# Taking all arithmetic off GpSimd in a three-block transformer kernel: rotation by transfers, probabilities on two engines, another order of gates

## The chip, the cores and the metric

The kernel runs on one core of a Trainium2 chip. A core has a matrix engine (TensorE, PE in the rows), a vector engine (VectorE, DVE), a scalar engine (ScalarE, ACT), GpSimd (POOL), and queues from which transfers between HBM and the on-chip memory are started; the queue of SyncE (SP) starts most of them. Each engine works through its own list of instructions in the order in which the program recorded them, and stands still when the instruction at the head of its list has to wait for another engine.

The metric is the time of one execution on the chip, in microseconds (us).

## The reference, cut to what matters

Three transformer blocks follow one another on a sequence of 512 tokens with 1024 features, all in fp32.

```python
# block 1: three branches on the normed input, mixed by gates
p = modulate(rms_norm(x, g1), sh1, sc1) @ w_in
q, k, v, a_dn, r, conv_in, sgu_in, gate_logit = split(p)
y_a = rms(gla_bidir(q, k, v, gates_f, gates_b, ...)) * silu(r) @ w_o_gla     # branch 0
y_b = silu(layer_norm(depthwise_conv(c1 * sigmoid(c2)))) @ w_o_conv          # branch 1
y_c = (su * spatial(layer_norm(sv))) @ w_o_sgu                               # branch 2
g = sigmoid(gate_logit)
x = x + g1 * ((g[0] * y_a + g[1] * y_b + g[2] * y_c) @ w_out);  x = x + g2 * swiglu(...)
# block 2, two layers
x = x + 0.5 * swiglu(x)
fq, fk, fv, ff, dq, dk, dv = split(rmsnorm(x) @ w_in)
o_f = softmax(fq @ fk.T / 8 + forget gates, causal) @ fv                     # 8 heads
dq, dk = rope(dq), rope(dk)          # t * cos + rotate_half(t) * sin
o_d = rms((softmax(dq1 @ dk1.T / 8) - lam * softmax(dq2 @ dk2.T / 8)) @ dv)  # 4 heads
x = x + concat(o_f, o_d) @ w_out;  x = x + 0.5 * swiglu(x)
# block 3: attention and a linear recurrence with gates side by side, then one projection
```

`rotate_half` takes the two halves of 32 features of a head and swaps them, with the sign of one turned.

## The kernel before, in words

**Layout.** Activations lie with features on the 128 partitions and the 512 tokens along the free axis, one buffer of 128x512 for 128 features (the names b in the rows). Each fp32 product is emulated by three passes on TensorE: an operand is split into a rounded part (hi) and the rest (lo), and hi·hi, hi·lo and lo·hi are added up in a PSUM bank (bk). `main_mm3` issues those three matmuls.

**The weight stream.** All weights come as 542 chunks of 128x1024 on the SP queue into `wraw` (three buffers). ScalarE casts a chunk into `whi`, and a subtraction, wraw − whi, makes `wlo`. It stands in `w_finish` (L506): on VectorE, or on GpSimd for chunks of odd number while `poolprep` is set, which it is in the two mixers of block 2 and in block 3.

**Main work and background work.** The recording code runs through the projections in order; these are the main matmuls. Everything else (gated linear attention, called GLA; attention heads; convolution; norms) is written as generators that are stepped (`tick`, L561) after each group of three main matmuls and put their own instructions in between. A generator stops at `sync()` (L430) until a modelled time has come, so that TensorE isn't given a matmul whose inputs are still being made. The modelled times come from `Clock` (L185): one clock for each engine, moved on by the `cost_*` functions (L209 to L237) whenever an instruction is recorded through the wrapper `Engine` (L241; all compute instructions therefore carry its line L260 in the profile). `idle()` moves TensorE's clock where no main matmul is left to put in. The order on each engine is thus fixed when the program is built, by the planner's costs; nothing is reordered on the chip.

**Block 1** (0 to about 860 us, then its feed-forward part until about 1396 us). `ORDER_1` (L1890) sets the order of main units: `r` are the inputs of GLA's output gate, `g` the gates of the three branches, `a` the rest of the modulation, `s` and `v` the two halves of the spatial branch, `between(b, ahead)` puts the products of branch b, each ahead of the gates of the next branch. GLA's heads (`gla_gate`, `gla_dir`, `gla_head`, L2051 to L2260) and the convolution (`conv_work`, L2275, one VectorE instruction for each of 31 taps of 8 buffers) are background work. The first product of branch 0 needs the last GLA head.

**Block 2's mixers** (`mixer2`, L1199; about 1600 to 1870 us and 2600 to 2870 us). `MIX_ORDER` runs the four differential heads (`diff(h)`), the values, and four pairs of forget-gate heads (`fox(j)`). `diff` makes q and k of a head: ScalarE copies four groups of 32 partitions out of PSUM to their rotated place (with the scale), VectorE multiplies the unrotated product by the cosines (`cosr`); later `rotated` (L1066) multiplies the rotated copy by the sines (`sinr`) on GpSimd and adds it there. `stack` (L774) splits the result and takes the low parts of each half-head (64 partitions) by subtractions on GpSimd. An attention head (`Pair`, L893) makes scores, exponentials, row sums, and in `probs` (L973) scales each row block by the reciprocal of its sum on VectorE; `turned` transposes and splits the probabilities, `products` multiplies with the values.

**Block 3** begins at about 3220 us and ends the program.

## Time and profile before

| what | us |
|---|---|
| median of 3 runs (3471.91 to 3474.83) | 3472.56 |
| the profiled execution | 3473.23 |
| its span | 3471.5 |

Over the span TensorE is busy 96%, VectorE 55%, ScalarE 40%, GpSimd 21%. These are averages over parts with very different loads, so the rows below go by stretch. A row of busy times by stretch reads: window in us from the start of the span, its length, then for PE, PEld (weight load), DVE, ACT and POOL the busy us and in brackets the instructions, then TensorE's granted clock as a share of full speed, the share of the transfer engines, GB/s. A row of waits reads: who waited, for whose result, us in all, times, the longest. A row of a group by shape reads: line, engine, operation, out<-in with shapes, count, busy us, mean ns, idle time before them and its releasers. A row of a tile reads: line, engine, operation, out<-in, count, duration in ns as shortest/median/longest. A row of the timeline or of the chain of waits begins with start and duration in us.

### The profile page before, as it was taken

To read this page: it belongs to the slowest core of one execution; us is meant where nothing else is said; L and a number is where in the kernel's file an instruction comes from. 1 tells how busy PE (TensorE), PEld (TensorE's weight loads), DVE (VectorE), ACT (ScalarE), POOL (GpSimd) and SP (SyncE) were. 2 spreads that over 40 slices of the span, in tenths; PEclk is the share of its full clock that TensorE was granted. 3 is DMA by queue.
4 is the path that set the end of the run, shared out by engine and by line. 5 is a ranking of instruction groups with operands and counts; after the bars stand their busy time and mean duration, and the time that the engine had idled before them with its cause. 6 is when DMAs were issued, how large, how long until landed. Compare 5 with 4: busy or idle time off the path is not lost.

```text
span 3471.5 us, 39465 instructions
## 1 busy us (share of the span) xinstructions
PE 3348.1 (96%) x15208; PEld 2757.0 (79%) x15208; DVE 1915.9 (55%) x3016; ACT 1373.7 (40%) x2220; POOL 718.9 (21%) x556
## 2 busy tenths in 40 slices
PE   7999989999999999999989999999999899999998
PEld 4887778887888888888767888888887678888787
DVE  5899887655333365433885443344334874433566
ACT  3325454333222332325864222222227753322465
POOL 0005221321000111104542110111017341111353
PEclk8999999999999999999999999999999999999999
DMA  5311115533222254332212222222332123222221
GB/s 199 103 67 60 50 68 187 177 115 106 96 97 97 93 171 159 102 115 97 67 61 86 97 96 97 92 97 97 112 109 76 43 76 107 97 94 95 79 85 49
DMA packets 110189, 345.00 MB, mean 99 GB/s; under 512 B 13424, under 2 KB 13680, under 8 KB 110000
## 3 DMA queue, kind: packets, MB, share of 16 engines
q1 hardware_dynamic: 84960, 296.78, 25.3%
q10 hardware_dynamic: 23760, 41.50, 3.8%
...
q14 instruction: 70, 0.57, 0.1%
...
## 4 chain that ended last, share of the span: by engine, by line
PE 48%; DVE 6%; ACT 3%; issue 1%; POOL 1%; POOLq 0%; DVEq 0%; ACTq 0%
PE bk L260 48%; DVE b L260 4%; ACT b L260 3%; DVE tinies L260 1%; DVE wlo L260 0%; ACT whi L260 0%; POOL b L260 0%; POOL wlo L260 0%; ACT L255 0%; POOLq L2841 0%; ACT bk L260 0%; ACT tinies L260 0%; DVEq L260 0%; DVE small L260 0%; ACTq L260 0%
## 5 line engine op out<-in xcount | busy, mean ns | idle before, releaser
L260 PE MATMUL bk<-b,whi 128*128 128x512 f32 (+1 forms) x8048 | 2504.9, 393 | 13.0 <-ACT b L260 7.6
L260 PEld LDWEIGHTS bk<-b,whi 128*128 128x128 f32 x8048 | 1504.9, 189 | 322.1 <-DVE b L260 10.2
L260 PE MATMUL bk<-b,wlo 128*128 128x512 f32 (+1 forms) x4024 | 1571.4, 391 | 13.5 <-DVE wlo L260 13.5
L260 POOL TENSOR_TENSOR b<-b,b 128x512 f32<-128x512 f32 (+2 forms) x381 | 527.3, 1392 | 2345.6 <-ACT b L260 1336.7
L260 DVE TENSOR_TENSOR wlo<-wraw,whi 128x1024 fp32r<-128x1024 f32 x495 | 648.2, 1311 | 529.7 <-ACT whi L260 528.7
L260 PEld LDWEIGHTS bk<-b,wlo 128*128 128x128 f32 x4024 | 760.3, 189 | 175.1 <-DVE wlo L260 16.5
L260 ACT CAST whi<-wraw 128x1024 fp32r<-128x1024 f32 x542 | 568.0, 1049 | 713.0 <-PE bk L260 416.3
L260 ACT CAST b<-b 128x512 fp32r<-128x512 f32 (+3 forms) x286 | 176.0, 619 | 521.3 <-POOL b L260 374.5
L260 DVE TENSOR_TENSOR b<-bk,b 128x512 f32<-128x512 f32 (+6 forms) x324 | 207.8, 657 | 251.5 <-PE bk L260 209.5
L260 DVE TENSOR_TENSOR b<-b,b 128x512 fp32r<-128x512 f32 (+3 forms) x250 | 180.9, 732 | 266.5 <-ACT b L260 264.0
L260 ACT ACTIVATE b<-b 128x512 f32<-128x512 f32 (+1 forms) x262 | 155.7, 607 | 295.7 <-DVE b L260 256.3
L260 DVE SCALAR_TENSOR_TENSOR b<-b,pvt,b 128x392 f32<-128x392 f32 (+7 forms) x296 | 237.3, 806 | 33.0 <-ACT b L260 26.4
L260 PE MATMUL bk<-whi,b 128*128 128x512 f32 x768 | 246.2, 396 | 2.6 <-ACT b L260 2.2
L260 PE MATMUL bk<-b,b 128*128 128x256 f32 (+6 forms) x1056 | 205.7, 337 | 28.3 <-DVE tinies L260 8.5
L260 PEld LDWEIGHTS bk<-b,b 128*128 128x128 f32 (+2 forms) x1056 | 171.9, 201 | 60.9 <-POOL b L260 17.4
L260 PEld LDWEIGHTS bk<-whi,b 128*128 128x128 f32 x768 | 146.0, 190 | 33.7 <-ACT b L260 2.7
L260 DVE SCALAR_TENSOR_TENSOR b<-b,small,b 128x512 f32<-128x512 f32 (+1 forms) x178 | 149.3, 840 | 19.5 <-ACT b L260 15.1
L260 POOL TENSOR_TENSOR wlo<-wraw,whi 128x1024 fp32r<-128x1024 f32 x47 | 118.0, 2510 | 202.3 <-ACT whi L260 170.7
L260 PE MATMUL bk<-cst,b 128*128 128x128 f32 (+1 forms) x776 | 112.7, 274 | 45.6 <-DVE b L260 38.1
L260 PEld LDWEIGHTS bk<-cst,b 128*128 128x128 f32 x776 | 98.5, 168 | 70.7 <-DVE b L260 50.0
L260 PE MATMUL bk<-wlo,b 128*128 128x512 f32 x384 | 151.0, 393 | 0.0
L260 ACT ACTIVATE b<-bk 128x512 f32<-128x512 f32 (+2 forms) x170 | 97.0, 571 | 106.0 <-PE bk L260 99.2
...
## 6 DMA issues: line engine op xcount, KB each, us to landing
wraw<-in_wst SPq DMA_DIRECT2D x542, 512.0 KB, 3.3
b<-in_ada1r ACTq DMA_DIRECT2D x64, 256.0 KB, 4.4
b<-in_ada ACTq DMA_DIRECT2D x48, 256.0 KB, 4.1
b<-in_ada SPq DMA_DIRECT2D x32, 256.0 KB, 5.3
xpark<-b ACTq DMA_DIRECT2D x16, 256.0 KB, 2.0
b<-xpark POOLq DMA_DIRECT2D x16, 256.0 KB, 5.6
b<-in_x SPq DMA_DIRECT2D x8, 256.0 KB, 5.7
b<-in_x ACTq DMA_DIRECT2D x8, 256.0 KB, 4.6
```

What stands on the lines that cost most here:

```text
L260: return f(*a, **kw)
```

## The change

No arithmetic is left on GpSimd. Every `nc.gpsimd` call that computes becomes the same call on VectorE: products and subtractions of GLA, the convolution's and the spatial branch's norms, sums of squares, `stack`, the product of the FFN, `poolprep`'s odd chunks (the switch is gone). Of its 560 rows GpSimd keeps 28: constants, memsets and the 16 transfers that bring x back. VectorE's instructions go from 3018 to 3534: 269 more of the kind b<-b,b 128x512, 80 of 64x512, 48 copies of 128x128, 47 chunks of `wlo`, 16 scalar-tensor-tensor with a PSUM operand (b<-bk,b, for the sines), 16 of 128x256 and some 60 small or single ones, less 22 scalings of probabilities. ScalarE's go from 2183 to 2136: 64 copies of 32x512 fewer, 22 scalings more. SP gets 64 transfers of 32x512 (64 KB each).

The rotation is now made after the sines: VectorE multiplies the product in PSUM by −s and the sines, four transfers move groups of 32 partitions to their rotated places, and a VectorE addition joins the two parts. `probs` gives a scaling to ScalarE where its modelled clock is behind VectorE's. The planner's clock no longer uses 0.5 for the two engines' sharing but 0.7, also for instructions that begin while the modelled GpSimd is busy. `ORDER_1` puts four gates of branch 2 ahead of branch 0's products. Block 3 waits with two kinds of unit until 8 buffers are free.

```diff
@@ class Clock
+        if shared and self.c["pool"] > t:
+            t += SHARED * min(self.c["pool"] - t, 1.4)
         self.c[name] = t + dur
         if name == "pool" and self.c["dve"] > t:
-            self.c["dve"] += 0.5 * min(dur, self.c["dve"] - t)
+            self.c["dve"] += SHARED * min(dur, self.c["dve"] - t)
...
+SHARED = 0.7
...
+    def copy_in(self, out, src):
+
+        t = self.clk.t
+        self.nc.sync.dma_start(out, src)
+        self.clk.t = t
+        return max(t, self.clk.now) + 2.2
...
-            eng = nc.gpsimd if self.poolprep and i % 2 else nc.vector
+            eng = nc.vector
             eng.tensor_sub(lo, src, hi.bitcast(F32))
...
-        nc.gpsimd.tensor_sub(lows[e].r[own[e] if keys else own[1 - e]], t.f[own[e]], out[e].f[own[e]])
+        k.nc.vector.tensor_sub(lows[e].r[own[e] if keys else own[1 - e]], t.f[own[e]], out[e].f[own[e]])
...
         for qb, o in part:
-            v = ss[0].f[:, o:o + qb * P + P]
-            ve.tensor_scalar(v, v, self.sm.f[:, 16 + qb:17 + qb], None, op0=ALU.mult)
+            v, r = ss[0].f[:, o:o + qb * P + P], self.sm.f[:, 16 + qb:17 + qb]
+            if k.clk.c["act"] < k.clk.c["dve"]:
+                k.act(v, v, AF.Copy, scale=r)
+            else:
+                ve.tensor_scalar(v, v, r, None, op0=ALU.mult)
...
@@ rotated
-        x, t = st["d" + name].pop(self.h)
-        yield from k.sync()
-        nc.gpsimd.tensor_mul(x.f, x.f, st["sinr"].f)
-        yield from k.sync()
-        nc.gpsimd.tensor_add(t.f, t.f, x.f)
+        x, t, at = st["d" + name].pop(self.h)
+        k.clk.t = max(k.clk.t, at)
+        yield from k.sync()
+        k.nc.vector.tensor_add(t.f, t.f, x.f)
...
@@ diff
-            x, t = k.blk(), k.blk()
-            for c in range(0, P, 32):
-                nc.scalar.mul(x.f[c:c + 32], b[c ^ 32:(c ^ 32) + 32], s)
+            y, x, t = k.blk(), k.blk(), k.blk()
+            nc.vector.scalar_tensor_tensor(y.f, b, -s, st["sinr"].f, op0=ALU.mult, op1=ALU.mult)
+            at = max(k.copy_in(x.f[c:c + 32], y.f[c ^ 32:(c ^ 32) + 32]) for c in range(0, P, 32))
             nc.vector.scalar_tensor_tensor(t.f, b, s, cosr.f, op0=ALU.mult, op1=ALU.mult)
             k.unbank(b)
-            st["d" + name][h] = x, t
+            k.free(y)
+            st["d" + name][h] = x, t, at
...
-ORDER_1 = (some("r", range(KT)) + some("g", range(KT), 0) + some("g", range(KT), 1) + some("a", [0]) + between(0, KT)
-           + between(1, KT) + some("v", range(2)) + some("s", range(KT)) + some("g", range(6), 2) + between(2, 6))
+ORDER_1 = (some("r", range(KT)) + some("g", range(KT), 0) + some("g", range(KT), 1) + some("a", [0])
+           + some("g", range(4), 2) + between(0, KT) + between(1, KT) + some("v", range(2)) + some("s", range(KT))
+           + some("g", range(4, 6), 2) + between(2, 6))
...
@@ gla_dir
-    nc.gpsimd.tensor_mul(qe.f, q.f, qe.f)
-    nc.gpsimd.tensor_mul(ke.f, kk.f, ke.f)
-    nc.gpsimd.tensor_mul(kd.f, kk.f, kd.f)
+    k.nc.vector.tensor_mul(qe.f, q.f, qe.f)
+    k.nc.vector.tensor_mul(ke.f, kk.f, ke.f)
+    k.nc.vector.tensor_mul(kd.f, kk.f, kd.f)
```

In the first mixer of block 2, GpSimd's list held, for the first differential head: the products with the sines, the two additions, one chunk of `wlo` and the four subtractions of `stack`.

```order
187 L260 TENSOR_TENSOR b_774_10300<-b_774_10300,b_770_10264 128x512
188 L260 TENSOR_TENSOR b_776_10339<-b_776_10339,b_770_10264 128x512
189 L260 TENSOR_TENSOR b_775_10301<-b_775_10301,b_774_10300 128x512
190 L260 TENSOR_TENSOR b_777_10340<-b_777_10340,b_776_10339 128x512
191 L260 TENSOR_TENSOR wlo_86<-wraw_80,whi_83 128x1024
192 L260 TENSOR_TENSOR b_780_10404<-b_775_10301,b_780_10404 64x512
193 L260 TENSOR_TENSOR b_781_10405<-b_775_10301,b_781_10405 64x512
194 L260 TENSOR_TENSOR b_784_10418<-b_777_10340,b_782_10416 64x512
195 L260 TENSOR_TENSOR b_785_10419<-b_777_10340,b_783_10417 64x512
```

In the changed kernel VectorE's list holds the same work at the same place. b_776 is the cosine part of q and b_779 that of k, b_775 and b_778 are the rotated sine parts that the transfers fill, and bk_66 is the next head's product.

```order
1464 L267 TENSOR_TENSOR wlo_88<-wraw_82,whi_85 128x1024
1465 L267 TENSOR_TENSOR b_776_10306<-b_776_10306,b_775_10305 128x512
1466 L267 SCALAR_TENSOR_TENSOR b_780_10381<-bk_66,b_770_10263 128x512
1467 L267 SCALAR_TENSOR_TENSOR b_782_10383<-bk_66,b_769_10262 128x512
1468 L267 TENSOR_TENSOR b_779_10346<-b_779_10346,b_778_10345 128x512
1469 L267 TENSOR_TENSOR wlo_86<-wraw_80,whi_83 128x1024
1470 L267 TENSOR_TENSOR b_783_10397<-b_776_10306,b_783_10397 64x512
1471 L267 TENSOR_TENSOR b_784_10398<-b_776_10306,b_784_10398 64x512
1472 L267 SCALAR_TENSOR_TENSOR b_789_10434<-bk_71,b_770_10263 128x512
1473 L267 SCALAR_TENSOR_TENSOR b_791_10436<-bk_71,b_769_10262 128x512
1474 L267 TENSOR_TENSOR b_787_10417<-b_779_10346,b_785_10415 64x512
1475 L267 TENSOR_TENSOR b_788_10418<-b_779_10346,b_786_10416 64x512
```

The additions and the subtractions now stand between weight chunks and the PSUM reads of the next head, in one list; the products with the sines have moved forward to the PSUM reads (rows 1466 and 1472).

On SP, which before had only weight chunks here, the rotation's transfers stand between the chunks.

```order
296 L257 DMA wraw_80<-in_wst 128x1024
297 L257 DMA b_775_10305<-b_774_10304 32x512 x4
298 L257 DMA wraw_81<-in_wst 128x1024
299 L257 DMA b_778_10345<-b_777_10344 32x512 x4
300 L257 DMA wraw_82<-in_wst 128x1024
301 L257 DMA b_781_10382<-b_780_10381 32x512 x4
302 L257 DMA wraw_80<-in_wst 128x1024
303 L257 DMA b_790_10435<-b_789_10434 32x512 x4
```

Each group of four waits for the product with the sines on VectorE, and the weight chunk behind it waits with it.

On TensorE at the end of GLA in block 1, before: the last transposes of a GLA head (128x128, with cst, the constants) stood directly ahead of branch 0's first product (bk_73<-b_203 and on, the output of GLA's head).

```order
1755 L260 MATMUL bk_71<-cst,b_259_3308 128x128 x2
1756 L260 MATMUL bk_71<-cst,b_266_3369 128x128 x2
1757 L260 MATMUL bk_67<-b_75_468,whi_85 128x512
1758 L260 MATMUL bk_67<-b_76_469,whi_85 128x512
1759 L260 MATMUL bk_67<-b_75_468,wlo_88 128x512
1760 L260 MATMUL bk_73<-b_203_2649,whi_83 128x512
1761 L260 MATMUL bk_73<-b_204_2650,whi_83 128x512
```

Now the same two transposes, and further down the first product (bk_70<-b_202). Between the two pieces stand 138 main matmuls.

```order
1714 L267 MATMUL bk_70<-cst,b_253_3207 128x128 x2
1715 L267 MATMUL bk_70<-cst,b_255_3257 128x128 x2
1716 L267 MATMUL bk_67<-b_65_325,whi_84 128x512
1717 L267 MATMUL bk_67<-b_66_326,whi_84 128x512
1718 L267 MATMUL bk_67<-b_65_325,wlo_87 128x512
```

```order
1852 L267 MATMUL bk_73<-b_75_468,whi_83 128x512
1853 L267 MATMUL bk_73<-b_76_469,whi_83 128x512
1854 L267 MATMUL bk_73<-b_75_468,wlo_86 128x512
1855 L267 MATMUL bk_70<-b_202_2601,whi_84 128x512
1856 L267 MATMUL bk_70<-b_203_2602,whi_84 128x512
```

The distance from the last transposes of this head to the product that needs its output went from three main matmuls to 138, of which the four gates make 96.

## Rows read from the trace of the kernel before

**Rows 1.** The page's line of busy time over the span.

```profile
PE 3348.1 (96%) x15208; PEld 2757.0 (79%) x15208; DVE 1915.9 (55%) x3016; ACT 1373.7 (40%) x2220; POOL 718.9 (21%) x556
```

**Rows 2.** Busy times by stretch; the columns are told above.

```profile
245.00:470.00 225.00, 202.55 (x963) 164.71 (x962) 201.41 (x261) 108.94 (x211) 89.25 (x72) 0.93 0.16 56
1600.00:1870.00 270.00, 247.81 (x1204) 204.01 (x1203) 193.97 (x462) 185.54 (x398) 132.69 (x103) 0.96 0.22 72
1870.00:2600.00 730.00, 730.00 (x3234) 605.00 (x3233) 282.72 (x318) 211.28 (x256) 79.57 (x60) 1.00 0.30 100
2600.00:2870.00 270.00, 242.75 (x1157) 199.03 (x1156) 188.22 (x456) 182.92 (x393) 131.39 (x102) 0.94 0.20 65
3360.00:3471.50 111.50, 98.22 (x479) 80.76 (x477) 73.75 (x180) 73.32 (x152) 44.73 (x41) 0.95 0.14 48
1700.00:1800.00 100.00, 86.50 (x457) 71.50 (x456) 86.55 (x266) 72.23 (x193) 39.69 (x42) 0.91 0.18 58
```

**Rows 3.** Waits of TensorE from 245 to 470 us.

```profile
PE bk L260 <- POOL b L260: 8.9, 5, 3.4
PE bk L260 <- ACT b L260: 7.8, 2, 7.4
```

**Rows 4.** Waits of TensorE from 1600 to 1870 us.

```profile
PE bk L260 <- DVE b L260: 17.4, 10, 6.2
```

**Rows 5.** Waits of TensorE from 2600 to 2870 us.

```profile
PE bk L260 <- DVE b L260: 15.6, 11, 2.9
PE bk L260 <- DVE wlo L260: 6.3, 3, 2.4
PE bk L260 <- DVE tinies L260: 5.1, 2, 4.9
```

**Rows 6.** Durations on VectorE, by tile, over the span (shapes at the end).

```profile
L260 DVE TENSOR_TENSOR b<-bk,b x324: 407/683/695, 177.4 to 3448.3; 128x512 f32<-128x512 f32 x109, 128x384 fp32r<-128x384 f32 x26, 64x512 f32<-64x512 f32 x12, 128x512 fp32r<-128x512 f32 x9
...
L260 DVE TENSOR_TENSOR wlo<-wraw,whi x495: 1160/1224/3190, 21.6 to 3436.3; 128x1024 fp32r<-128x1024 f32 x165
...
L260 DVE SCALAR_TENSOR_TENSOR tinies<-tinies,small x32: 210/562/2352, 1649.2 to 2736.5; 128x1 f32<-128x1 f32 x32
L260 DVE SCALAR_TENSOR_TENSOR b<-b,tinies,b x32: 351/750/2797, 1649.8 to 2736.8; 128x512 f32<-128x512 f32 x8, 128x384 f32<-128x384 f32 x8, 128x256 f32<-128x256 f32 x8, 128x128 f32<-128x128 f32 x8
```

**Rows 7.** Two groups of GpSimd by shape, over the span.

```profile
L260 POOL TENSOR_TENSOR b<-b,b 128x512 f32<-128x512 f32 x285 | 404.3, 1428 | 2013.8 <-ACT b L260 1032.6 <-DVE b L260 896.0 <-issue 57.9
...
L260 POOL TENSOR_TENSOR b<-b,b 64x512 fp32r<-64x512 f32 x80 | 107.6, 1346 | 44.5 <-ACT b L260 18.3 <-issue 16.4 <-PE bk L260 3.4
```

**Rows 8.** Timeline of VectorE from 2658 to 2673 us.

```profile
2659.95 1.33 DVE L260 SCALAR_TENSOR_TENSOR tinies<-tinies,small 128x1 f32<-128x1 f32 x1
2661.31 2.80 DVE L260 SCALAR_TENSOR_TENSOR b<-b,tinies,b 128x512 f32<-128x512 f32 x1
...
2670.81 1.43 DVE L260 SCALAR_TENSOR_TENSOR b<-b,tinies,b 128x128 f32<-128x128 f32 x1
```

**Rows 9.** Timeline of GpSimd from 2656 to 2673 us.

```profile
2656.59 4.67 POOL L260 TENSOR_TENSOR b<-b,b 128x512 f32<-128x512 f32 x3
2661.22 2.35 POOL L260 TENSOR_TENSOR wlo<-wraw,whi 128x1024 fp32r<-128x1024 f32 x1
2663.64 8.45 POOL L260 TENSOR_TENSOR b<-b,b 64x512 fp32r<-64x512 f32 x6
```

**Rows 10.** ScalarE's copies for the rotation, by shape, over the span.

```profile
L260 ACT ACTIVATE b<-bk 32x512 f32<-32x512 f32 x64 | 37.7, 589 | 4.1 <-PE bk L260 3.3
```

**Rows 11.** Transfers: kind, count, size of one, median us from issue to landing.

```profile
b<-xpark POOLq DMA_DIRECT2D x16, 256.0 KB, 5.6
...
b<-in_aup ACTq DMA_DIRECT2D x6, 64.0 KB, 2.1
```

**Rows 12.** Two pieces of the chain of waits in block 3's end.

```profile
3371.20 2.42 POOL wlo L260
...
3440.88 2.39 POOL wlo L260
```

More of the change, by code (lines that the diff above doesn't have):

```diff
@@ L197, in now, with add @@
         return self.c["pe"]
-    def add(self, name, dur):
+    def add(self, name, dur, shared=False):
         t = self.t - self.LAT if self.src == name else self.t
         t = max(self.c[name], t, self.c["pe"])
+        if shared and self.c["pool"] > t:
+            t += SHARED * min(self.c["pool"] - t, 1.4)
         self.c[name] = t + dur
         if name == "pool" and self.c["dve"] > t:
-            self.c["dve"] += 0.5 * min(dur, self.c["dve"] - t)
+            self.c["dve"] += SHARED * min(dur, self.c["dve"] - t)
         self.t = self.c[name] + self.LAT
@@ L238, in cost_pool, with in_psum @@
     return 0.06 + 1.0e-3 * width(out) if op == "memset" else max(0.5, 0.1 + 2.7e-3 * width(out))
+def in_psum(x):
+    return getattr(getattr(x, "tensor", None), "space", None) == bass.MemoryType.PSUM
 class Engine:
@@ L258, in g @@
                 out = a[0] if a else kw["out"]
-                self._clk.add(self._n, self._cost(op, out, a, kw))
+                shared = self._n == "dve" and not any(in_psum(x) for x in (*a, *kw.values()))
+                self._clk.add(self._n, self._cost(op, out, a, kw), shared)
                 return f(*a, **kw)
@@ L683, in feed @@
         else:
-            k.nc.gpsimd.tensor_add(self.acc.f, t.f, self.acc.f)
+            k.nc.vector.tensor_add(self.acc.f, t.f, self.acc.f)
             k.free(t)
@@ L746, in ffn @@
             k.unbank(pu)
-            nc.gpsimd.tensor_mul(u.f, t.f, u.f)
+            k.nc.vector.tensor_mul(u.f, t.f, u.f)
         hi, lo = k.rblk(), k.rblk()
@@ L925, in turned @@
         if c0:
-            nc.gpsimd.tensor_copy(hi.r[:, 0:c0], k.c("mask")[:, 0:c0])
-            nc.gpsimd.tensor_copy(lo.r[:, 0:c0], k.c("mask")[:, 0:c0])
+            nc.vector.tensor_copy(hi.r[:, 0:c0], k.c("mask")[:, 0:c0])
+            nc.vector.tensor_copy(lo.r[:, 0:c0], k.c("mask")[:, 0:c0])
         yield from k.sync()
@@ L973, in probs @@
     def probs(self, part, ss):
-        ve = self.k.nc.vector
+        k, ve = self.k, self.k.nc.vector
         rs = self.sm.f[:, 16 + part[-1][0]:17 + part[0][0]]
@@ L993, in finish @@
         if "ga" in st:
-            nc.gpsimd.tensor_mul(t.f, t.f, st["ga"][j].f)
+            k.nc.vector.tensor_mul(t.f, t.f, st["ga"][j].f)
             k.free(st["ga"][j])
@@ L1216, in mixer2 @@
     nc.scalar.dma_start(sinr.f, k.a["rope"][:, 1, :])
-    nc.gpsimd.tensor_mul(cosr.f, cosr.f, norm.bc)
-    nc.gpsimd.tensor_mul(sinr.f, sinr.f, norm.bc)
+    k.nc.vector.tensor_mul(cosr.f, cosr.f, norm.bc)
+    k.nc.vector.tensor_mul(sinr.f, sinr.f, norm.bc)
     z, t, cum = k.blk(), k.blk(), k.rblk()
@@ L1312, in out_proj @@
     k.drain()
-    k.poolprep = False
     for m in range(NOUT):
@@ L1370 @@
 H3 = 4
+NEED3 = 8
 def plan3():
@@ L1481, in feed @@
             else:
-                k.nc.gpsimd.tensor_add(parts[0].f, t.f, parts[0].f)
+                k.nc.vector.tensor_add(parts[0].f, t.f, parts[0].f)
                 k.free(t)
@@ L1528, in make @@
         if m % 2:
-            nc.gpsimd.tensor_mul(xa.f, xa.f, self.bc.f)
+            k.nc.vector.tensor_mul(xa.f, xa.f, self.bc.f)
         else:
@@ L1721, in lru_rest @@
         t = k.blk()
-        nc.gpsimd.tensor_mul(t.f, r.f, r.f)
+        k.nc.vector.tensor_mul(t.f, r.f, r.f)
         yield from k.sync()
@@ L1787, in lru @@
             r, i = gs
-            nc.gpsimd.tensor_mul(y.f, y.f, i.f)
+            k.nc.vector.tensor_mul(y.f, y.f, i.f)
             k.free(i)
@@ L1831, in block3 @@
     for kind, i in ORDER_3:
+        if kind in "sg":
+            k.need(NEED3)
         if kind == "x":
@@ L2083, in ctx_state @@
     last = t.f[:, 0:1] if s else t.f[:, n - 1:n]
-    nc.gpsimd.tensor_sub(w.f[:, 0:n], t.f[:, 0:n], last.to_broadcast([P, n]))
+    k.nc.vector.tensor_sub(w.f[:, 0:n], t.f[:, 0:n], last.to_broadcast([P, n]))
     k.act(w.f[:, 0:n], w.f[:, 0:n], AF.Exp, scale=-1.0 / 16)
-    nc.gpsimd.tensor_mul(w.f[:, 0:n], w.f[:, 0:n], st["ck"][h])
+    k.nc.vector.tensor_mul(w.f[:, 0:n], w.f[:, 0:n], st["ck"][h])
     yield from k.sync()
@@ L2159, in gla_dir @@
     f, l = pairs(kd.f)[:, :, s], pairs(qe.f)[:, :, 1 - s]
-    nc.gpsimd.tensor_mul(f, f, chunk[:, :, 1 - s:2 - s].to_broadcast([P, 4, 64]))
-    nc.gpsimd.tensor_mul(l, l, chunk[:, :, s:s + 1].to_broadcast([P, 4, 64]))
+    k.nc.vector.tensor_mul(f, f, chunk[:, :, 1 - s:2 - s].to_broadcast([P, 4, 64]))
+    k.nc.vector.tensor_mul(l, l, chunk[:, :, s:s + 1].to_broadcast([P, 4, 64]))
     yield from k.sync()
@@ L2230, in gla_head @@
     k.clk.t = old
-    nc.gpsimd.tensor_scalar(ss, ss, 1.0 / 256, EPS1, op0=ALU.mult, op1=ALU.add)
+    nc.vector.tensor_scalar(ss, ss, 1.0 / 256, EPS1, op0=ALU.mult, op1=ALU.add)
     k.rsqrt(y, ss, u)
@@ L2394, in sgu_norm @@
         v = t.f[:, 8 + tt:9 + tt]
-        nc.gpsimd.tensor_scalar(v, s.f[:, 13:14], EPS1, None, op0=ALU.add)
-        nc.gpsimd.tensor_copy(t.f[:, tt:tt + 1], s.f[:, 12:13])
+        nc.vector.tensor_scalar(v, s.f[:, 13:14], EPS1, None, op0=ALU.add)
+        nc.vector.tensor_copy(t.f[:, tt:tt + 1], s.f[:, 12:13])
         k.free(s)
@@ L2403, in sgu_norm @@
             nc.vector.tensor_scalar(x.f, x.f, t.f[:, tt:tt + 1], t.f[:, 16 + tt:17 + tt], op0=ALU.subtract, op1=ALU.mult)
-            nc.gpsimd.tensor_mul(x.f, x.f, st["lng"][half].f)
-            nc.gpsimd.tensor_add(x.f, x.f, st["lnb"][half].f)
+            k.nc.vector.tensor_mul(x.f, x.f, st["lng"][half].f)
+            k.nc.vector.tensor_add(x.f, x.f, st["lnb"][half].f)
             if tt % 2:
@@ L2427, in sgu_mix @@
     k.unbank(b)
-    nc.gpsimd.tensor_mul(su.f, t.f, su.f)
+    k.nc.vector.tensor_mul(su.f, t.f, su.f)
     k.free(t)
@@ L2677, in product @@
         else:
-            nc.gpsimd.tensor_add(yacc[m].f, yacc[m].f, g.f)
+            k.nc.vector.tensor_add(yacc[m].f, yacc[m].f, g.f)
             k.free(g)
```

11 lines of the change are left out of this document (4 added, 7 removed).

## The prediction

> **What bounds the kernel now.** I read the busy line first: TensorE works 3348.1 of 3471.5 us, so 123.4 us are idle, and no other engine comes near it [rows 1]. Then the busy times by stretch, because an average over parts with different limits tells nothing of a change in some of them [rows 2]. From 1870 to 2600 us (feed-forward work) TensorE is busy all 730 us at a granted clock of 1.00: there a moved instruction on another engine can cost or gain nothing as long as its results come in time. The idle time lies in GLA (245 to 470 us: 225 − 202.55 = 22.5 us), the two mixers (270 − 247.81 = 22.2 and 270 − 242.75 = 27.3) and the end of block 3 (111.5 − 98.22 = 13.3). It costs more than itself: the granted clock there is 0.93, 0.96, 0.94 and 0.95 as a mean of the levels 1.2 and 2.4 GHz, it falls after idle time, and a stretch with mean c loses up to (1 − c) of its busy time beside the idle time. With that, GLA loses 22.5 + 0.07 × 202.55 = 36.6 us, the mixers 22.2 + 0.04 × 247.81 = 32.1 and 27.3 + 0.06 × 242.75 = 41.8, the end 13.3 + 0.05 × 98.22 = 18.2: 128.7 us that other engines' work can change. The first 245 us hold nothing that the edit touches much, and I leave them and the short remaining stalls out.
>
> Last I read whom TensorE waits for there. In GLA: GpSimd 8.9 us in five waits, ScalarE 7.8 in two, one of them 7.4 [rows 3]. In the first mixer VectorE's b for 17.4 of the 22.2 us [rows 4], in the second VectorE for 15.6 + 6.3 + 5.1 = 27.0 of 27.3 [rows 5]. So in the mixers GpSimd is not what TensorE waits for by name; the edit adds work to the engine that is.
>
> **Why moving work onto the waited-for engine can help.** VectorE is slow there for a reason that leaves with GpSimd. An operation that reads PSUM takes 683 ns at the median and never more than 695 [rows 6]. One that reads only on-chip memory varies: a chunk of wlo 1160 at the least and 3190 at the most, the one-column product that prepares a differential head's probabilities 210 to 2352, the wide one behind it 351 to 2797 [rows 6]. A stretch of the second mixer shows when [rows 8, 9]: from 2659.95 to about 2672 VectorE runs four such pairs, with only two short reciprocals between them; the eight operations add up to 12.0 us (1.33 + 2.80 for the first pair; the last operation, 128x128, takes 1.43), while GpSimd works without a break for 15.5 us (4.67 + 2.35 + 8.45). Alone the pairs would take 4 × 0.21 + (0.75 + 0.62 + 0.49 + 0.35) = 3.1 us by the shortest and middle durations of rows 6 (0.62 and 0.49 are interpolated by width). GpSimd's ten operations there are priced on VectorE at 3 × 0.69 + 1.22 + 6 × 0.69 = 7.4 us (0.69 for 512 columns, whatever the partitions; 1.22 for a chunk). Both engines together thus need 10.5 us in one list where they took 12.0 side by side.
>
> The Trainium skill (SBUF — State Buffer, "SBUF: two separate sides") says that VectorE and GpSimd share a port pair which one instruction holds to its end, among others for a VectorE operation with two on-chip inputs against a GpSimd one that reads on-chip memory. By that rule operations of two on-chip inputs should stretch and those with a PSUM input not, and the trace agrees (up to 3190 against at most 695 ns [rows 6]).
>
> **The change part by part.**
>
> *Moved arithmetic.* GpSimd's mean for 128x512 is 1428 ns and for 64x512 1346 [rows 7]; on VectorE 690, a ratio of 0.48 to 0.51; a chunk 2.35 [rows 9] against 1.22. At 0.49 the first mixer's 132.69 us of GpSimd [rows 2] become 65 us of VectorE, the second's 131.39 become 64, GLA's 89.25 become 44, the end's 44.73 become 22. Against that goes the relief. It is at least nothing, and at most the example's rate, 8.9 us of excess in 15.5 us of GpSimd = 0.57, for all of GpSimd's time, 76 us in a mixer. Much of VectorE's work there reads PSUM and is not relieved, so I take 0.3: 40 us in a mixer, 27 in GLA, 13 in the end. VectorE's busy time then goes to 194 + 65 − 40 = 219 and 188 + 64 − 40 = 212 of 270 us, in GLA to 201 + 44 − 27 = 218 of 225, and in the end to 83 of 111.5. GLA is the tight one; its fill was 201.41 / 225 = 0.90 already. Its operations there are scans and taps of the convolution which fill in whatever time is left and are due later (the second half of block 1), so I let it slip rather than stop.
>
> *Rotation.* 64 copies of ScalarE go, 37.7 us in all [rows 10], 19 us in each mixer; the two GpSimd products for q and k of a head become 16 VectorE operations with a PSUM operand, 16 × 0.69 = 11 us, 5.5 in each mixer (they don't suffer contention, and the additions and the subtractions of the halves are in the 65 us above). The 64 transfers of 64 KB are new between weight chunks on SP. The nearest rows: 64 KB from HBM land in 2.1 us, 256 KB from the place where x is parked in 5.6 [rows 11]. The planner counts on 2.2. So each of 16 additions comes between 0 and 5.6 − 2.2 = 3.4 us late, 0 to 54 us for VectorE's list, since everything behind a waiting addition waits, the chunks' subtractions among them. I take 0.5 us each, 8 us, near the row of the same size, and half of it at TensorE: +4. A group of four that waits for its product holds back the next weight chunk on SP by as long; three chunks are in buffers, so I cost that at nothing, and if the buffers run dry it would show as waits for whi.
>
> *Probabilities.* 22 of 104 scalings go to ScalarE, 0.42 us each at the median shapes: less than 5 us per mixer off VectorE, on an engine that gets 19 us free. Part of what hides the rotation's 5.5.
>
> *Order of gates.* Between the last GLA transposes and the first product that needs GLA's output stand 138 main matmuls instead of three. At 730 / 3234 = 0.226 us [rows 2] that is 31 us of cover, where ScalarE's 7.4 us wait [rows 3] and those behind it now fall. What is late next is the convolution, whose taps share VectorE with the moved work; its products come at the end of branch 0's. I charge +3 (between 0 and its own share of one such wait, 7.4).
>
> *Block 3's buffers and the end.* The wait for eight buffers only moves units behind others; nothing by itself. Two chunks on GpSimd stand on the chain of waits, 2.42 and 2.39 us [rows 12]; on VectorE 1.22 each.
>
> **The sum.** GLA: the 8.9 us of waits for GpSimd go, with the clock that hangs on idle time 8.9 × 36.6 / 22.5 = 14.5, and half of ScalarE's 7.8, 3.9: −18. Mixers: the example's 12.0 us become 10.5 if all moved work stands ahead of the result that is waited for (12% less) and 3.1 if none does (74%). I take 35%, below the middle, because VectorE's fill goes up to 0.8: 32.1 × 17.4 / 22.2 × 0.35 = −9 and 41.8 × 27.0 / 27.3 × 0.35 = −14.5. The end: a third of 18.2, −6, of which the two chunks are 2.4. Together −47.5; +4 +3 of new waits: −40.5. From the profiled execution's 3473.2 that is 3432.7; the median of the runs lies 0.7 below that execution, so 3432.
>
> **The rivals.**
>
> *A, VectorE becomes the bound of the mixers (slower).* If the relief is near nothing, the first mixer's list holds 194 + 65 + 5.5 − 4.6 = 260 us and the second's 188 + 64 + 1 = 253. The highest fill that a stretch of rows 2 shows is 0.90; the mixers then take 260 / 0.90 = 289 and 281 us, +19 and +11. Less GLA's 14.5, with nothing won at the end: +15.5, 3488. It decides from the point where VectorE's busy time in a mixer exceeds 243 us (0.90 × 270), that is with a relief under about 15 us; for it speaks that in the dense 100 us from 1700 VectorE is busy 86.55 already, more than TensorE's 86.50 [rows 2]; against it the stretched durations of rows 6. The skill speaks for A (Perfetto Trace Analysis, "Optimizing Scalar/DVE Operations"): between GpSimd and VectorE, which share a port, moving operations might not help. By that sentence alone the sum would be that of A or C; the trace shows up to 2.6 times the duration for a chunk beside GpSimd [rows 6], and I hold with the rows.
>
> *B, late transfers.* At the upper bound of 54 us on VectorE, half at TensorE, +27 in place of +4: 3455. For it: SP's queue also carries 512 KB chunks; against: transfers are busy 0.20 to 0.22 of the time in the mixers [rows 2].
>
> *C, the waits change owner only.* GpSimd's waits become VectorE's of the same length: 3472 within 7 us.
>
> *D, most of it goes.* Of the 128.7 us the mixers' relief reaches 74% of its waits and GLA's stalls go with the 31 us of cover: 0.74 × (25.2 + 41.3) + 36.6 + 9 = 95, 3378.
>
> **How the numbers follow.** Forecast 0.46 (3405 to 3455), A 0.17, B 0.12, C 0.11, D 0.14. A difference under 0.2%, 7 us, can't be told from none. Faster: forecast, B and D, 0.72; same: C, 0.11; slower: A, 0.17. The range goes down to 3388, which leaves out half of D, and up to 3483, which leaves out two thirds of A.
>
> **What would show it.** Right: wlo and the wide products [rows 8] at their shortest durations with hardly any spread; GpSimd's waits gone; VectorE's busy time in the mixers near 215 us and the mixers 10 to 15 us shorter; no wait of TensorE of 5 us near the end of GLA. Wrong: VectorE over 243 us of 270 in a mixer (A); VectorE idle for transfers ahead of the 16 additions by more than a microsecond each (B); a convolution that comes late by over 10 us in block 1; waits of the old length under VectorE's name (C).

## The result, and the profile after

The changed kernel takes 3415.11 us (median of 4 runs, 3414.29 to 3416.99), the one before 3472.23 beside it: a ratio of 0.9835 with a 95% interval of 0.9822 to 0.9848, 57 us faster where 40 were forecast. The time lies inside the range, and the forecast case was the one that came; but two of its terms, the rotation and block 3, came out with the wrong sign, as the runs below show.

The page's line of busy time of the changed kernel, against [rows 1]:

```profile
PE 3324.9 (97%) x15208; PEld 2741.6 (80%) x15208; DVE 2042.5 (60%) x3532; ACT 1348.2 (39%) x2173; POOL 9.3 (0%) x24
```

Stretches are cut at the starts of the same weight chunks' subtractions. In the mixers that is the same work on TensorE as in [rows 2] (1204 and 1157 matmuls); GLA's stretch holds 1032 where it held 963, because background work falls elsewhere. Busy times of the changed kernel by stretch: GLA, first mixer, the feed-forward work between, second mixer, the end of block 3.

```profile
249.00:463.00 214.00, 205.34 (x1032) 169.69 (x1032) 182.78 (x323) 113.54 (x231) 0.00 (x0) 0.99 0.17 57
1579.00:1831.00 252.00, 242.06 (x1204) 199.41 (x1203) 210.83 (x556) 169.57 (x372) 4.37 (x8) 0.99 0.26 84
1831.00:2559.00 728.00, 728.00 (x3225) 603.14 (x3224) 314.17 (x377) 210.26 (x253) 0.00 (x0) 1.00 0.30 100
2559.00:2799.00 240.00, 230.78 (x1157) 190.61 (x1156) 205.28 (x550) 165.40 (x366) 4.36 (x8) 0.99 0.26 83
3308.00:3414.00 106.00, 87.27 (x421) 72.31 (x419) 78.32 (x197) 64.76 (x138) 0.00 (x0) 0.91 0.14 50
```

TensorE's idle time fell from 22.2 to 9.9 us in the first mixer and from 27.3 to 9.2 in the second, and the granted clock there went from 0.96 and 0.94 to 0.99. The end went the other way: 18.7 us idle at 0.91. The last window of the end in [rows 2] begins earlier; cut at the same chunk, the kernel before had 13.3 us idle there, at 0.94:

```profile
3371.00:3471.50 100.50, 87.22 (x428) 71.53 (x427) 71.63 (x172) 62.58 (x135) 37.26 (x35) 0.94 0.15 53
```

In the first mixer VectorE does more work (210.8 us of 252, against 194.0 of 270) and yet is waited for less. Its durations show why; by tile, against [rows 6]:

```profile
L267 DVE TENSOR_TENSOR wlo<-wraw,whi x542: 1161/1225/1227, 21.4 to 3394.4; 128x1024 fp32r<-128x1024 f32 x181
...
L267 DVE SCALAR_TENSOR_TENSOR tinies<-tinies,small x32: 213/219/223, 1620.3 to 2669.8; 128x1 f32<-128x1 f32 x32
L267 DVE SCALAR_TENSOR_TENSOR b<-b,tinies,b x32: 350/552/752, 1620.5 to 2670.1; 128x512 f32<-128x512 f32 x8, 128x384 f32<-128x384 f32 x8, 128x256 f32<-128x256 f32 x8, 128x128 f32<-128x128 f32 x8
```

The longest chunk went from 3190 to 1227 ns, the longest small product from 2352 to 223. TensorE's waits in the first mixer of the changed kernel, against [rows 4], and in GLA, against [rows 3]:

```profile
PE bk L267 <- DVE b L267: 8.9, 9, 4.5
PE bk L267 <- DVE wlo L267: 0.6, 1, 0.6
PE bk L267 <- ACT b L267: 0.3, 1, 0.3
```

```profile
PE bk L267 <- DVE b L267: 7.8, 8, 2.2
PE bk L267 <- ACT b L267: 0.8, 1, 0.8
```

And the transfers that VectorE waits for, over the span (all waits of its own operations for the rotation):

```profile
DVE b L267 <- DMA b<-b: 1.7, 3, 1.3
```

### The profile page after: what moved, and what is told of

Same layout as the page of the kernel before. It is cut to its first block, busy times and chain, and to the rows that moved or that the text cites. A ratio compares the mean times of both kernels' runs of the same rounds, so it can differ in the third digit from the quotient of the medians.

```text
span 3414.0 us, 39098 instructions
## 1 busy us (share of the span) xinstructions
PE 3324.9 (97%) x15208; PEld 2741.6 (80%) x15208; DVE 2042.5 (60%) x3532; ACT 1348.2 (39%) x2173; POOL 9.3 (0%) x24
## 5 line engine op out<-in xcount | busy, mean ns | idle before, releaser
L267 DVE TENSOR_TENSOR wlo<-wraw,whi 128x1024 fp32r<-128x1024 f32 x542 | 661.5, 1222 | 554.5 <-ACT whi L267 552.6
L267 DVE TENSOR_TENSOR b<-b,b 128x512 f32<-128x512 f32 (+4 forms) x615 | 407.6, 672 | 183.3 <-ACT b L267 149.3
L267 ACT ACTIVATE b<-b 128x512 f32<-128x512 f32 (+2 forms) x261 | 155.1, 608 | 280.5 <-DVE b L267 268.2
L267 DVE SCALAR_TENSOR_TENSOR b<-b,pvt,b 128x392 f32<-128x392 f32 (+7 forms) x296 | 204.9, 696 | 32.0 <-ACT b L267 25.5
L267 PE MATMUL bk<-b,b 128*128 128x128 f32 (+6 forms) x1056 | 191.8, 320 | 17.5 <-DVE b L267 9.6
L267 PEld LDWEIGHTS bk<-b,b 128*128 128x128 f32 (+2 forms) x1056 | 159.2, 188 | 44.1 <-ACT b L267 13.7
L267 DVE SCALAR_TENSOR_TENSOR b<-b,small,b 128x512 f32<-128x512 f32 (+1 forms) x178 | 133.5, 750 | 22.3 <-ACT b L267 19.0
L267 PEld LDWEIGHTS bk<-cst,b 128*128 128x128 f32 x776 | 98.7, 168 | 50.8 <-DVE b L267 34.5
L267 ACT COPY b<-bk 128x512 f32<-128x512 f32 (+5 forms) x130 | 65.7, 535 | 118.1 <-PE bk L267 116.9
L267 ACT ACTIVATE b<-b,tinies 128x512 f32<-128x512 f32 (+3 forms) x182 | 100.3, 560 | 29.3 <-DVE tinies L267 29.0
L267 DVE TENSOR_TENSOR b<-b,bk 128x512 f32<-128x512 f32 x64 | 43.9, 686 | 110.2 <-PE bk L267 102.9
```

Of the source, the lines that this page charges most:

```text
L267: return f(*a, **kw)
```

## The experiments

The table has the length of each stretch in the profiled execution of each kernel, in us, from the start of one chunk's subtraction to that of another (chunks counted from 0; the last column of stretches goes to TensorE's last matmul), and the median of its runs. Two kernels with the same lists in a stretch differ there by up to 2.6 us (175.7 and 178.3 in block 3), so smaller differences say nothing, and a sum of two stretches is uncertain by more. In GLA's stretch the kernels with the arithmetic on VectorE run some 64 more matmuls than the others (1032 and 968 in arith_only and before), so against the kernel before only the sum of the first two columns is to be read.

| kernel | GLA 32–55 | 55–120 | mixer 251–282 | mixer 416–445 | block 3 507–533 | end | median |
|---|---|---|---|---|---|---|---|
| before | 224.7 | 399.8 | 270.3 | 270.3 | 168.8 | 96.5 | 3472.2 |
| changed | 214.0 | 389.7 | 251.6 | 240.2 | 177.9 | 101.4 | 3415.1 |
| arith_only | 213.9 | 402.8 | 262.5 | 255.5 | 175.7 | 97.0 | 3450.8 |
| rot_only | 222.9 | 400.4 | 264.0 | 250.7 | 169.0 | 96.6 | 3447.3 |
| order_only | 223.1 | 403.0 | 270.4 | 270.2 | 168.7 | 96.5 | 3474.8 |
| old_order | 213.5 | 402.8 | 251.2 | 241.3 | 176.1 | 101.1 | 3430.0 |
| old_rot | 213.5 | 391.3 | 264.9 | 256.1 | 175.8 | 102.0 | 3444.0 |
| old_probs | 213.5 | 388.2 | 254.4 | 243.0 | 177.9 | 98.7 | 3417.1 |
| beside | 213.5 | 389.8 | 278.5 | 267.4 | 176.6 | 102.1 | 3471.0 |
| beside_write | 213.5 | 388.1 | 254.4 | 243.2 | 175.7 | 101.9 | 3419.8 |
| act_load | 213.5 | 389.8 | 256.7 | 246.9 | 178.3 | 101.3 | 3429.3 |
| rot_act | 213.5 | 389.7 | 267.5 | 258.9 | 176.5 | 101.2 | 3449.3 |
| gp_lru | 213.4 | 388.2 | 251.0 | 241.3 | 169.4 | 95.6 | 3404.8 |
| best | 213.9 | 389.8 | 251.7 | 241.7 | 169.6 | 95.2 | 3402.4 |

**1. Only the moved arithmetic (arith_only).** The parts that are undone, against the changed kernel:

```diff
-            at = max(k.copy_in(x.f[c:c + 32], y.f[c ^ 32:(c ^ 32) + 32]) for c in range(0, P, 32))
+            for c in range(0, P, 32):
+                nc.scalar.mul(x.f[c:c + 32], b[c ^ 32:(c ^ 32) + 32], s)
...
-           + some("g", range(4), 2) + between(0, KT) + between(1, KT) + some("v", range(2)) + some("s", range(KT))
+           + between(0, KT) + between(1, KT) + some("v", range(2)) + some("s", range(KT))
...
-            if k.clk.c["act"] < k.clk.c["dve"]:
...
-            k.need(NEED3)
```

> The changed kernel with three parts undone and block 3's wait for buffers left out: rotation by ScalarE's copies again (its product and addition on VectorE), all probabilities on VectorE, the old order of gates. So of the change only the move of GpSimd's arithmetic to VectorE is left. Theory of relief (VectorE is stretched by GpSimd's work beside it, and that ends): the two mixers, 541 us together before and 492 in the changed kernel, come to 490 to 510; wlo at 1160 to 1230 ns; the whole at 3425 to 3440. Rival (rotation by transfers and the split of probabilities make the mixers shorter by taking work from ScalarE): the mixers stay at 530 or more, the whole at 3450 or more.

3450.79 us, ratio 0.9934 (0.9919 to 0.9949). The mixers took 518.0 us: 22.6 less than before, not 30 to 50. Neither theory's figure for the mixers was met, and the whole just reaches the rival's 3450: relief is real (no chunk takes longer than 1228 ns here), and is less than half of the mixers' 48.8.

**2. Idle GpSimd work beside (beside).**

```diff
             eng.tensor_sub(lo, src, hi.bitcast(F32))
+            if self.beside:
+                g, u = self.raw.gpsimd, self.load
+                g.tensor_mul(u[:, 0:1], hi[:, 0:1].bitcast(F32), u[:, 0:1])
+                for _ in range(3):
+                    g.tensor_mul(u, u, u)
```

> The changed kernel with idle work on GpSimd in block 2's mixers: behind each chunk of weights, once it is prepared, one product of one column that reads whi and three products of 128x512 in a buffer of its own, that nobody reads; about 4.3 us per chunk, 31 and 29 chunks, some 130 us in each mixer, as much as GpSimd had before. The lists of all other engines are those of the changed kernel. Theory of relief: wlo and the wide products stretch again (wlo to 2 us and more at the longest), VectorE's busy time in a mixer grows by 20 to 40 us and each mixer by 10 to 30; the whole 3435 to 3475. Rival (the gain came from the other order of the lists): VectorE's durations grow but the mixers stay within 5 us each, the whole under 3425.

3470.99 us, all that the change had won; the mixers 54.1 us longer with the same lists. The theory of relief has its direct proof: nothing but GpSimd's work was added. The chunk's durations, by tile, and GpSimd's own work by shape:

```profile
L267 DVE TENSOR_TENSOR wlo<-wraw,whi x542: 1161/1225/2060, 21.2 to 3446.8; 128x1024 fp32r<-128x1024 f32 x181
```

```profile
L541 POOL TENSOR_TENSOR load<-load 128x512 f32<-128x512 f32 x186 | 233.3, 1254 | 14.6
```

That it costs more here than moving the arithmetic won is no contradiction: VectorE carries the moved work as well, which I take for the reason; no run tests it.

**3. Idle GpSimd work that reads nothing (beside_write).**

```diff
-                for _ in range(3):
-                    g.tensor_mul(u, u, u)
+                for _ in range(7):
+                    g.memset(u, 0.0)
```

> As the kernel with idle work on GpSimd beside the mixers, but instead of three products of 128x512 behind each chunk seven fills of 128x512 with a constant, which read no buffer. Theory (what stretches VectorE is that both engines read on-chip memory): wlo stays at 1230 ns and the mixers within 5 us of the changed kernel, the whole under 3425. Rival (any GpSimd work beside stretches VectorE): wlo to 1.8 us or more, the mixers longer by 20 us or more together, the whole over 3435.

3419.76 us; the mixers 5.8 us longer than in the changed kernel, a little over the bound expected. GpSimd was as busy as in the run before it (229.8 against 233.3 us), and no chunk was stretched:

```profile
L267 DVE TENSOR_TENSOR wlo<-wraw,whi x542: 1159/1225/1228, 22.0 to 3398.2; 128x1024 fp32r<-128x1024 f32 x181
```

```profile
L541 POOL MEMSET load<- 128x512 f32 x434 | 229.8, 530 | 25.1
```

So it is not GpSimd's being busy that stretches VectorE, but its reading. Another rival falls with it: in both runs ScalarE's next cast sometimes waits until the idle work lets a `whi` buffer go, and it waits longer in the cheap run (36.7 us) than in the dear one (20.1). The Trainium skill says the same (SBUF — State Buffer, "SBUF: two separate sides"): a VectorE operation with two on-chip inputs contends only with a GpSimd operation that reads on-chip memory. The two runs agree with it.

**4. The rotation undone (old_rot)**, the first edit of experiment 1 alone, with the product with the sines and the addition on VectorE.

> The changed kernel with the rotation alone undone (64 ScalarE copies, product with the sines and addition on VectorE). Theory of relief: VectorE has the same number of operations, ScalarE 19 us more in each mixer; the mixers longer by 0 to 8 us together, the whole 3415 to 3424. Rival (the transfers carry the mixers' gain): mixers longer by 20 us or more, the whole over 3435.

3443.99 us, the mixers 29.2 us longer: the rival's figure. The rotation, which I had priced at +4, carries as much of the mixers' gain as the relief, or more. TensorE waits little for ScalarE by name here, so I looked one step back, at what VectorE waits for. From 1597 to 1717 us, where the differential heads are made:

```profile
DVE b L267 <- ACT b L267: 18.8, 10, 6.4
```

In the changed kernel, in the same work (1589 to 1697 us):

```profile
DVE b L267 <- PE bk L267: 4.2, 5, 1.6
DVE b L267 <- ACT b L267: 3.6, 6, 0.8
```

The same row in the kernel before (1613 to 1733 us), and in the kernel before with the rotation by transfers (rot_only of experiment 7, 1611 to 1720 us):

```profile
DVE b L260 <- ACT b L260: 28.2, 14, 7.8
```

```profile
DVE b L260 <- ACT b L260: 4.1, 7, 0.7
```

The timeline of ScalarE in the kernel with the old rotation, and then that of VectorE beside it (start, duration; in brackets the idle time before it):

```profile
1623.95 2.40 ACT L267 ACTIVATE b<-bk 32x512 f32<-32x512 f32 x4
1626.38 1.05 ACT L267 CAST whi<-wraw 128x1024 fp32r<-128x1024 f32 x1
1627.34 3.13 ACT L267 CAST b<-b 64x512 fp32r<-64x512 f32 x5
...
1632.37 2.39 ACT L267 ACTIVATE b<-bk 32x512 f32<-32x512 f32 x4
```

```profile
1626.38 0.69 DVE L267 SCALAR_TENSOR_TENSOR b<-bk,b 128x512 f32<-128x512 f32 x1 [2.71 <-ACT b L267]
...
1634.79 0.69 DVE L267 SCALAR_TENSOR_TENSOR b<-bk,b 128x512 f32<-128x512 f32 x1 [6.40 <-ACT b L267]
1635.40 1.21 DVE L267 TENSOR_TENSOR wlo<-wraw,whi 128x1024 fp32r<-128x1024 f32 x1
```

ScalarE works almost without a break, and the four copies stand behind the casts of the head before. VectorE's product with the cosines begins 0.03 us after the copies end, both times: the program lets it wait for the semaphore that the last copy raises. Behind it, the second time, a chunk's subtraction waits in VectorE's list. ScalarE's copies thus hold VectorE, and with it the weights. In these 46 us (1597 to 1643) ScalarE is busy 39.92 us; in the 40 us of the changed kernel (1589 to 1629) 27.65:

```profile
1597.00:1643.00 46.00, 42.16 (x181) 33.84 (x180) 27.36 (x42) 39.92 (x64) 0.00 (x0) 0.96 0.22 69
```

```profile
1589.00:1629.00 40.00, 39.71 (x193) 33.05 (x192) 35.02 (x78) 27.65 (x54) 0.00 (x0) 1.00 0.37 112
```

**5. Idle copies on ScalarE (act_load).**

```diff
             y, x, t = k.blk(), k.blk(), k.blk()
+            for c in range(0, P, 32):
+                k.raw.scalar.mul(k.load[c:c + 32], k.load[c:c + 32], s)
```

> The changed kernel with 64 copies of 32x512 on ScalarE in a buffer of their own that nobody reads, at the place in its list where the rotation's copies stood (four for each q and k of a differential head). The lists of the other engines are those of the changed kernel; the rotation goes on by transfers. Theory (the rotation gains because ScalarE, which casts each chunk of weights, was full while the heads' q and k are made): some 19 us more of ScalarE in each mixer, whi and so wlo late, the two mixers (492 us) longer by 15 to 30 us together, nearly as in the kernel with the old rotation (521), the whole 3430 to 3446. Rival (the gain comes from the order of VectorE's and TensorE's lists, which the planner made differently once the copies were gone, or from the shorter path from PSUM to the sum): under 6 us together, the whole under 3422.

3429.33 us, the mixers 11.8 us longer: between the two. The time of the copies on ScalarE, with nobody waiting for them, explains some two fifths of the 29.2.

**6. The rotation by ScalarE with the changed kernel's lists (rot_act).**

```diff
-            at = max(k.copy_in(x.f[c:c + 32], y.f[c ^ 32:(c ^ 32) + 32]) for c in range(0, P, 32))
+            for c in range(0, P, 32):
+                k.raw.scalar.copy(x.f[c:c + 32], y.f[c ^ 32:(c ^ 32) + 32])
+            at = max(k.clk.t, k.clk.now) + 2.2
```

> The changed kernel with its sines before the rotation, but the rotation itself made by four ScalarE copies of 32x512 instead of four transfers; the lists of TensorE and VectorE are those of the changed kernel, only ScalarE has the copies in addition, and they wait there for VectorE's product. The idle copies cost 11.8 us in the mixers, the whole undoing of the rotation 29.2. Theory (what the idle copies don't explain, 17 us, is the other order of VectorE's and TensorE's lists): the mixers 10 to 18 us longer than in the changed kernel together, the whole 3427 to 3435. Rival (it is copies on ScalarE that wait in its list and hold what stands behind them): 24 us or more, the whole 3439 or more.

3449.30 us, the mixers 34.6 us longer: the rival's figure, and not that of my theory of the planner's order. With TensorE's and VectorE's lists unchanged, the copies cost even more than undoing the edit. They wait in ScalarE's list (first row, 1580 to 1860 us; L1268 is their line), and what stands behind them comes late: VectorE's wait for `whi` in the first mixer (1582 to 1850 us), then the same in the changed kernel (1579 to 1831 us).

```profile
ACT b L1268 <- DVE b L267: 10.9, 5, 5.4
```

```profile
DVE wlo L267 <- ACT whi L267: 19.9, 11, 4.2
```

```profile
DVE wlo L267 <- ACT whi L267: 8.2, 5, 4.2
```

Part of it is this kernel's own: its copies wait for VectorE's product, while those of the kernel before waited for the matmuls. How the 17 us between 11.8 and 29.2 divide among VectorE's waits for copies and the planner's other choices (with the old rotation it also gives ScalarE 8 more scalings) isn't separated. VectorE's waits for ScalarE's b point to the first: in the first mixer 12.7 us in the changed kernel, 22.2 with the idle copies, 38.9 with the old rotation.

**7. Transfers alone on the kernel before (rot_only).**

```diff
-        nc.gpsimd.tensor_mul(x.f, x.f, st["sinr"].f)
...
-            for c in range(0, P, 32):
-                nc.scalar.mul(x.f[c:c + 32], b[c ^ 32:(c ^ 32) + 32], s)
...
+            nc.vector.scalar_tensor_tensor(y.f, b, -s, st["sinr"].f, op0=ALU.mult, op1=ALU.mult)
+            at = max(k.copy_in(x.f[c:c + 32], y.f[c ^ 32:(c ^ 32) + 32]) for c in range(0, P, 32))
```

> The kernel before with the rotation by transfers alone: product with the sines on VectorE out of PSUM, four transfers, the addition still on GpSimd. Theory (the gain of the rotation is its own): the mixers (541 us before) shorter by 15 to 35 us together, the whole 3440 to 3458. Rival (it needs GpSimd out of the way): shorter by under 8 us, the whole over 3465.

3447.30 us, ratio 0.9926 (0.9910 to 0.9943); the mixers 25.9 us shorter with GpSimd still at work (it has lost only the 16 products with the sines). Relief (22.6) and rotation (25.9) are two gains that very nearly add up: 48.5 against 48.8 for all of the change.

**8. The old order of gates (old_order) and the new one alone (order_only).** Both edits are those of `ORDER_1`, put into the other kernel.

> The changed kernel with the old order of gates in block 1. If the cover of 138 main matmuls is what shortened GLA: chunks 32 to 120 (245 to 830 us) longer by 8 to 15 us, with a TensorE wait of 5 us or more near 450 us, the whole 3423 to 3430. Rival (GLA is shorter because GpSimd's share of its chain is gone): longer by under 4 us, the whole under 3419.

> The kernel before with the new order of gates alone, GpSimd's arithmetic kept. Theory (the order gives 13 us of TensorE work between GLA and the products that need it, whoever does the arithmetic): chunks 55 to 120 (399.8 us before) shorter by 8 to 15, all else as before, the whole 3458 to 3466. Rival (the order pays only because VectorE has the moved work): within 3 us of before.

The first took 3430.04 us, 15 more than the changed kernel; the second 3474.75, no gain (ratio 1.0007, 0.9998 to 1.0017). The time fits the first theory of old_order, but not the place: chunks 55 to 120 are longer by 13.1 us and GLA not at all. ScalarE's 7.4 us wait [rows 3] had gone with the arithmetic alone (0.8 us are left in arith_only) and stands as before with the order alone. What the new order covers are waits that the moved arithmetic itself brings: from chunk 55 to 120 TensorE is idle 8.1 us in the kernel before, 19.5 with the old order, 10.0 in the changed kernel. Its waits in the kernel with the old order from 500 to 545 us:

```profile
PE bk L267 <- ACT b L267: 4.7, 1, 4.7
PE bk L267 <- DVE b L267: 3.8, 2, 3.1
PE bk L267 <- DVE tinies L267: 1.8, 1, 1.8
```

**9. Probabilities on VectorE (old_probs)**, the third edit of experiment 1 alone.

> The changed kernel with all scalings of probabilities on VectorE. Theory (VectorE is the engine that the mixers wait for, and ScalarE has room): the mixers longer by 2 to 8 us together, the end of block 3 the same or shorter by up to 4, the whole 3413 to 3422. Rival (the scalings on ScalarE delay its casts and exponentials): the mixers the same or shorter, the whole 3405 to 3414.

3417.05 us (3414.67 to 3425.79), not to be told from the changed kernel. By stretch the mixers are 5.6 us longer and the end 2.7 shorter, in both as the theory had it, each near what a single profile can tell.

**10. Block 3's products back on GpSimd (gp_lru).**

```diff
-        k.nc.vector.tensor_mul(t.f, r.f, r.f)
+        nc.gpsimd.tensor_mul(t.f, r.f, r.f)
...
-        k.nc.vector.tensor_mul(y.f, y.f, u.f)
+        nc.gpsimd.tensor_mul(y.f, y.f, u.f)
...
-            k.nc.vector.tensor_mul(y.f, y.f, i.f)
+            nc.gpsimd.tensor_mul(y.f, y.f, i.f)
```

In the changed kernel block 3 has a TensorE wait of 5.1 us at 3214. The timelines of ScalarE, then of VectorE there:

```profile
3213.55 1.28 ACT L261 ACT_TABLE_LOAD   x1
3214.85 3.58 ACT L267 ACTIVATE b<-bk,pvt 128x512 f32<-128x512 f32 x6
```

```profile
3216.15 0.69 DVE L267 TENSOR_TENSOR b<-b,b 128x512 f32<-128x512 f32 x1 [3.32 <-ACT b L267]
3216.76 1.22 DVE L267 TENSOR_TENSOR wlo<-wraw,whi 128x1024 fp32r<-128x1024 f32 x1
3217.89 1.89 DVE L267 TENSOR_TENSOR b<-b,b 128x512 f32<-128x512 f32 x3
```

The first moved product waits 3.32 us for ScalarE's sigmoid, which waits for a table load; the chunk and the rest stand behind it in one list, among them the low part of a convolution for which TensorE waits (3218.49 to 3219.17 us, in the last row). On GpSimd it had waited beside them.

> The changed kernel with three kinds of product in block 3's recurrence back on GpSimd (y times i, r squared, y times u; 12 operations of 128x512). In the changed kernel the first of them waits on VectorE for ScalarE's sigmoid with the low part of the last convolution and a chunk of wlo behind it, and TensorE waits 5.2 us there. Theory (that wait is a queue behind a waiting instruction): the 5.2 us go, block 3 from chunk 507 (279 us) shorter by 5 to 10 us, the whole 3405 to 3411. Rival (block 3 is longer because VectorE has more to do): no shorter than 2 us, or longer.

3404.80 us, ratio 0.9804 (0.9789 to 0.9818). The waits of TensorE from 3170 to 3240 us went from 5.1 to 0.5 us, and block 3 from chunk 507 on is 14.3 us shorter, more than expected. The waits, first in the changed kernel, then in this one:

```profile
PE bk L267 <- DVE b L267: 5.1, 1, 5.1
```

```profile
PE bk L267 <- DVE b L267: 0.5, 1, 0.5
```

And the busy times from chunk 507 to 533, again first in the changed kernel:

```profile
3130.50:3308.50 178.00, 167.82 (x755) 139.22 (x755) 105.89 (x181) 91.56 (x133) 0.40 (x4) 0.94 0.23 77
```

```profile
3131.30:3300.80 169.50, 163.97 (x758) 136.27 (x758) 105.63 (x180) 92.14 (x137) 17.98 (x16) 0.97 0.25 81
```

Of the 14.3 us, 8.5 lie here: TensorE is idle 10.2 and 5.5 us, and the granted clock is 0.94 and 0.97. VectorE is as busy in both (105.89 and 105.63 us), so the rival doesn't explain it. The other 5.8 us lie in the end, where none of the twelve products stands; what shortened it isn't shown.

**11. Both (best).** That kernel, and in block 3's attention alone all scalings on VectorE:

```diff
-            if k.clk.c["act"] < k.clk.c["dve"]:
+            if not isinstance(self, Moba) and k.clk.c["act"] < k.clk.c["dve"]:
```

> The changed kernel with block 3's twelve products of the recurrence on GpSimd and, in block 3's attention only, all scalings of probabilities on VectorE; the mixers keep the split. Parts add up if block 3 from chunk 533 on takes 93 to 95 us (95.6 with the products alone) and the whole 3400 to 3404; if the scalings there only cost because VectorE had the products as well, nothing is won: 3404 to 3407.

3402.43 us, ratio 0.9798 (0.9784 to 0.9813), the fastest of all, 70 us under the kernel before. Against gp_lru it is no measurable step: 95.2 and 95.6 us in the end.

## Why the prediction was right, and where it was wrong

| term | forecast | measured | from |
|---|---|---|---|
| GLA and the order, with +3 for the convolution | −15 | −20.8 (arithmetic −7.8, order −13.0) | stretch 32–120: changed and arith_only, minus before |
| mixers, relief | −23.5 | −22.6 | arith_only |
| rotation | +4 | −25.9 to −29.2 | rot_only, old_rot |
| probabilities in the mixers | 0 | −5.6 | old_probs |
| block 3 | −6 | +14.0 | 507 to the end |

**Relief in the mixers: right in mechanism and in size.** The 35% was chosen below the middle of 12 and 74%, so part of the agreement is luck; that VectorE with more work is waited for less is what the stretched rows [rows 6, 8] had said, and experiments 2 and 3 show the cause. VectorE's busy time, 210.8 and 205.3 us, is near the 215 that the prediction named, and far from the 243 from which rival A decided. The mixers came out 18.7 and 30.1 us shorter, beyond the 10 to 15 each that the prediction gave as the sign of being right; what is over comes from the next terms. The other rule that I weighed (the Trainium skill, Perfetto Trace Analysis, "Optimizing Scalar/DVE Operations": moving work between the two that share a port might not help) doesn't hold in the mixers here: −22.6 us of 541.

**Rotation: the step that failed.** The prediction counted VectorE's operations, the transfers and their lateness, and put the 19 us that ScalarE loses in each mixer at nothing ("an engine that gets 19 us free"), without giving a reason. ScalarE's 185.54 us of 270 [rows 2] leave room, but they are the mean of a stage. Where q and k of the heads are made ScalarE was nearly full (39.92 us of 46 in old_rot), and what waited behind its copies were VectorE's PSUM reads and the weight casts. Copies that nobody waits for give 11.8 us of it; how the rest divides stays open. The feared side didn't come: the transfers land in 2.0 us at the median, and VectorE waits 1.7 us for three of them. Rival B is out.

**GLA and the order: near in the sum, wrong in the reason.** I had put 14.5 us to GpSimd's waits and half of ScalarE's wait to the credit of the order. ScalarE's wait went with the arithmetic, which is worth 7.8 us from chunk 32 to 120; alone the order wins nothing. The line "what is late next is the convolution" pointed to waits after GLA (whether they are the convolution's isn't traced), but I charged them as a cost when the new order was what covered them (13.1 us). Nor was GLA the tight stretch: VectorE is busy 182.78 us of 214 there, not 218.

**Block 3: wrong sign.** I took a third of the losses as won, with two GpSimd chunks on the chain in it, and costed the rest as work. Of the moved products, the first costs by its place: it waits for ScalarE and holds everything behind it. The prediction said of the rotation's additions that everything behind a waiting one waits, and didn't ask the same of the recurrence's products. Experiment 10 gives 14.3 us back, 8.5 of them where these products stand. The arithmetic alone (arith_only) costs 7.4 us from chunk 507 on; the other 6.6 of the 14.0 are not separated, and the wait for eight buffers was not run by itself.

That the total fell inside the range is thus partly luck. The miss in it, 17 us, is the sum of larger ones: 29 us too little won in the mixers (48.8 against 19.5), nearly all of it the rotation's and the probabilities' (together 26.2 from arith_only to the changed kernel, so the single figures overlap), and 6 in block 1, against 20 too much in block 3; the other stretches have the remaining 2.
